# Output projection by seven products of quarters, with weight sums made by adding transfers

## The chip, the cores and the metric

The kernel runs on one core of one Trainium2 chip. The metric is the device time of one execution in microseconds; the kernel before takes 1031.3 us (median of 3 runs, 1031.29 to 1032.03).

The engines have these names: PE multiplies matrices (PEld is its weight load), DVE and ACT work element by element on 128 partitions, POOL does the same more slowly and also issues transfers that can add to what lies at their target, and SP issues plain transfers. Each engine takes its instructions strictly in its own order.

## The reference, cut to what matters

One decoder layer over 512 tokens of width 1024: three token-mixing branches (attention, pooling, state space), gated and summed to `merged`, an output projection, and a gated feed-forward block with its own norm.

```
merged = gates[:, :, 0] * y_a + gates[:, :, 1] * y_b + gates[:, :, 2] * y_c
x = x + merged @ w_o[i]
x = x + conv_ffn(rmsnorm(x, ln2_g[i]), ffn_w_up[i], ffn_conv_w[i], ffn_conv_b[i], ffn_w_down[i])
return rmsnorm(x, final_g)
```

`w_o` is 1024 x 1024, `merged` is 512 x 1024. All values are float32. The kernel splits each operand into a high part (rounded to PE's fp32r) and a low part (the rest), and a product is the sum of high x high, high x low and low x high (`mm3`): three matmuls for each block of 128 rows of the summed dimension.

## The kernel before

The program is a list of jobs. A job has a piece of weights (1 MB at most), a body with its matmuls, and what becomes of the result. While job n multiplies, the weights of job n+1 get their low part (DVE, `low`, line 215), those of job n+2 are cast to their high part (ACT, `cast`, line 195, in two halves), and those of job n+3 are fetched (SP, line 183). So PE's input passes SP, ACT and DVE in turn, one job apart. PE, ACT, DVE and POOL run in the order in which the program was written down (`manual_schedule`); `step()` marks the places in that order where work from other lists (`waiting`, `running`) is put in. The order of the transfers on SP is a scheduler's.

Around the change the jobs are these:

- The third branch (`branch_jobs(2, w_c, ..., last=True)`): four jobs of 48 matmuls, each for two blocks m of 128 columns of `merged`, all 512 tokens wide and transposed. After each block DVE multiplies the product by the gate (line 1265) and adds it to the sum of the other branches (1266), ACT casts the sum to its high part (1269), DVE makes the low part (1270).
- The output projection (`wo_jobs`): for each pair of token blocks (0, 1 and then 2, 3), for each half h of the 1024 output columns, two jobs of 24 matmuls, one for each half of the summed dimension. DVE adds the result to x (line 1291). After half 0 `norm_early` takes the row's squares (ACT) and the product with the norm weights (POOL, line 441). After half 1 `norm_late` finishes the norm: squares (ACT), weights (DVE 450), variance (451), square root (ACT 452), reciprocal and one refinement (454 to 456), scaling of both halves (464). PE then turns the block (`norm_turn`, line 430), ACT and DVE copy it to `uh2`, `ul2`, the input of the feed-forward block.
- The first up-projection jobs (`opening`, line 1493) begin with the token blocks 0 and 1, take in blocks 2 and 3 in the middle, and set off the low parts of their own weights late (`job.late`).

The kernel already uses a scheme of seven products of quarters instead of eight in other places (`sevens` for parts of the input projection, `sevens_down` for the down projection): the tokens are halved (LO, HI), the blocks of the summed dimension are taken in even and odd ones, the output columns are halved. `sums_of` makes the four sums on the side of the tokens and their high and low parts, in three steps that `step()` sets off one after the other.

Of the kernel before, what the change touches and what calls it, by code (L numbers as in the profile page):

```python
# [10 lines left out]
F32 = mybir.dt.float32  # L11
F32R = mybir.dt.float32r
# [71 lines left out]
def trunk(ctx: ExitStack, tc, out, x, rel_bias, ln1_g, w_in, b_gate, w_a, pool_w, pool_scale, w_b,  # L84
# [23 lines left out]
    def T(name, dt=F32, shape=(P, S)):  # L108
        return big.tile(list(shape), dt, name=name, tag="t")
# [323 lines left out]
            act.copy(hh, pv)  # L433
            dve.tensor_sub(ul[:, 4 * h:4 * h + 4, tb * P:(tb + 1) * P], pv, hh.bitcast(F32))

    def norm_early(t, g):

        ss, v0, xg = small("ss", [P, 1]), cpool.tile([P, 1], F32, name=f"v0_{len(V0)}"), T("xg")
        squares(act, t, ss)
        dve.tensor_scalar(v0, ss, 1.0 / D, EPS, OP.mult, OP.add)  # L440
        pool.tensor_tensor(xg, t, g[:, :S], OP.mult)
        V0.append(v0)
        return v0, xg

    def norm_late(t, g, v0, outs, both=False):

        ss, v, sq, r, rt = (small(n, [P, 1]) for n in ("ss", "v", "sq", "r", "rt"))
        squares(act, t, ss)
        xg = T("xg")
        dve.tensor_tensor(xg, t, g[:, S:], OP.mult)  # L450
        dve.scalar_tensor_tensor(v, ss, 1.0 / D, v0, OP.mult, OP.add)
        act.activation(sq, v, AF.Sqrt)
        yield xg
        dve.reciprocal(r, sq)
        dve.scalar_tensor_tensor(rt, r, v, r, OP.mult, OP.mult)
        dve.tensor_scalar(rt, rt, -0.5, 1.5, OP.mult, OP.add)
        if both:
            dve.tensor_tensor(r, r, rt, OP.mult)
            (_, a), (_, b) = outs(xg)
            dve.tensor_scalar(a, a, r, None, OP.mult)  # L460
            act.mul(b, b, r)
            return
        for o, src in outs(xg):
            dve.tensor_scalar(o, src, r, rt, OP.mult, OP.mult)
# [793 lines left out]
    def branch_jobs(b, w, parts, nk, last=False, more=()):  # L1258
        def evac(m, ps):
            if b == 1:  # L1260
                MG[m] = T("yo")
                act.copy(MG[m], ps)
                return
            s = SG[b, m]
            dve.tensor_tensor(s, s, ps, OP.mult)
            (dve if last else pool).tensor_tensor(MG[m], MG[m], s, OP.add)
            if last:
                h, l = T("mgh", F32R), T("mgl", F32R)
                act.copy(h, MG[m])
                dve.tensor_sub(l, MG[m], h.bitcast(F32))  # L1270
                MH[m] = (h, l)

        return jobs_a(w, 0, 8, lambda k: parts[k][0], lambda k: parts[k][1], nk, evac,
                      width=256 if nk > 4 else 512, more=more)


    X1 = {}
    nxt = {}
    late, late_split = [], []

# [4 lines left out]
                t = X1[tb, h] = T("x1")  # L1285
                sp.dma_start(t, x[tb * P:(tb + 1) * P, h * S:(h + 1) * S])

    def wo_jobs(pair, h):
        def evac(tb, ps):
            t = X1[tb, h]  # L1290
            dve.tensor_tensor(t, t, ps, OP.add)
            if h == 0:
                nxt[tb] = norm_early(t, nxt["g2"])
                return
            if "uh" not in nxt:
                nxt["uh"] = upool.tile([P, KD, S], F32R, name="uh2", tag="uh")
                nxt["ul"] = upool.tile([P, KD, S], F32R, name="ul2", tag="ul")
            v0, xg0 = nxt[tb]
            us = [T("u0"), T("u1")]
            it = norm_late(t, nxt["g2"], v0, lambda xg1: ((us[0], xg0), (us[1], xg1)))  # L1300
            next(it)

            def rest():
                next(it, None)
                yield
                norm_turn(us, nxt["uh"], nxt["ul"], tb)

            if pair == 0:
                r = rest()
                next(r)  # L1310
                running.append(after(1, r))
            elif tb == 2:
                r2 = rest()
                next(r2)
                late.append(r2)
            else:
                late.append(rest())
                late_split.pop(0)()

        return jobs_b(lambda k0, k1: [wsrc(w_o, k0, k1, h * S, h * S + S)], S,  # L1320
                      lambda k, tb: MH[k][0][:, tb * P:(tb + 1) * P],
                      lambda k, tb: MH[k][1][:, tb * P:(tb + 1) * P], KD, evac,
                      blocks=(2 * pair, 2 * pair + 1), turn_over=pair == 1 and h == 1)


    ACTS = {}
# [235 lines left out]
    def program():  # L1562
        yield from jobs_a(w_in, C_POOL, 8, uhk, ulk, KD, pool_evac)
        yield Call(lambda: waiting.append(rows_of_bias()))
        yield from v_jobs(0)
        yield from qk_jobs(0)
        yield from pool_out_job()
        yield Call(lambda: attend(0))
        yield Call(lambda: waiting.insert(3, ssd_prep()))
        for i, job in enumerate(branch_jobs(1, w_b, YB, 8, more=range(7))):  # L1570
            if i == 3:
                yield Call(lambda: running.extend(after(p, sums_of_u(p)) for p in range(4)))
            yield job
        load, pair = v_pair()
        Q = lambda i: (C_Q + 384 + i * P, lambda: q_sink(1, i))
        K = lambda i: (C_K + 384 + i * P, lambda: k_sink(1, i))
        G = lambda i, left: (C_GATE + D + i * P, lambda: gate_sink(1, i, left))
        BC = lambda lo, hi, width: jobs_a(w_in, C_XBC + lo * P, hi - lo, uhk, ulk, KD,
                                          lambda m, ps: xbc_evac(lo + m, ps), width)
        loads, s = zip(  # L1580
            set_of_sevens((G(2, True), G(3, True)), (G(4, False), G(5, False)), "a"),
            set_of_sevens((Q(0), Q(1)), (K(0), K(1)), "c", (0.125, 0.125)),
            set_of_sevens((Q(2), G(0, True)), (K(2), G(1, False)), "a", (0.125, 1.0)))
        yield Call(load)
        yield from BC(8, 10, 256)
        yield from gate_jobs(1, 6, 8)
        pair[5].then, pair[6].then, s[0]["four"].then = loads
        yield from pair
        spare = BC(10, 12, P)
        for i, n in ((0, "one"), (0, "five"), (0, "two"), (0, "three"), (0, "six"), (1, "one"),  # L1590
                     (0, "seven"), (1, "five"), (0, "four"), (1, "three"), (1, "two"), (1, "six"),
                     (2, "one"), (1, "seven"), (2, "five"), (1, "four"), (2, "three"), (2, "two"),
                     (2, "six"), (2, "seven"), (2, "four")):
            if (i, n) in ((2, "seven"), (2, "four")):
                yield next(spare)
            yield s[i][n]
        yield Call(settle)
        yield Call(lambda: attend(1))
        yield from BC(0, 8, 256)
        yield Call(ssd_start)  # L1600
        yield from qk_jobs(2)
        yield Call(lambda: attend(2))
        yield Call(lambda: fill([after(2, combine())]))
        yield from gate_jobs(0)
        many = {"a": branch_jobs(0, w_a, AO, 3), "g": gate_jobs(2),
                "Z": z_jobs(0), "z": z_jobs(1)}
        for token in MIX:
            if token in many:
                yield next(many[token])
            else:  # L1610
                yield Call(lambda i=int(token): waiting.append(y_norm(i)))
        yield Call(finish)
        yield from branch_jobs(2, w_c, YT, 8, last=True)
        yield Call(load_x1)
        for pair in range(2):
            for h in range(2):
                yield from wo_jobs(pair, h)
            if pair == 0:
                yield Call(ff_cols)
        first, between, _ = sevens_down(0)  # L1620
        second_, last_, opened = sevens_down(1, keep=True)
        extra = {EARLY + i: between[w] for i, w in enumerate(
            ("two", "one", "five", "three", "six", "seven", "four"))}
        extra.update({LATE + i: last_[w] for i, w in enumerate(("two", "one", "five", "six"))})
        for i, job in enumerate(up_jobs()):
            yield job
            if i == EARLY - 3:
                yield Call(first)
            if i == LATE - 1:
                yield Call(second_)  # L1630
            if i in extra:
                yield extra[i]
        yield Call(lambda: fin.setdefault("g", grow(final_g)))
        yield Call(finish)
        yield from down(last_, opened)
# [181 lines left out]
NBIG = 54  # L1817
MORE = 2
SPLIT = 4
MIX = "ZZ0zz1ggggaa"  # L1820
SSD_ORDER = ((0, 0, 1), (1, 0, 1), (0, 1, 1), (2, 0, 1), (1, 1, 1), (3, 0, 1), (2, 1, 1), (3, 1, 1))
WARM = 19
EARLY, LATE = 8, 18
# [29 lines left out]
```

## Time and profile before

| | before |
|---|---|
| median of the runs | 1031.3 us |
| profiled execution | 1029.93 us |
| its span | 1028.2 us |
| granted PE clock (mean) | 0.999 |
| PE busy | 1019.2 us (99%) |
| DVE busy | 698.6 us (68%) |
| ACT busy | 485.1 us (47%) |
| POOL busy | 161.7 us (16%) |
| third branch | 579.6 to 623.1 us |
| output projection | 623.1 to 669.0 us |

The span counts from the first to the last instruction of the profiled execution; the execution's own time holds a little more. In the lists of instructions a row gives the start in us, the duration (of all in the row, where it ends in x2 or more), the engine, the line, the operation, output and inputs, the shape, and in brackets how long the engine had been idle and what ended that. A matmul row's duration includes its way through the array; what counts is the distance from start to start.

### The profile page before, as it was taken

The numbers are of one execution on the slowest core, as the hardware profiler recorded it, in microseconds if no ns is written. First come the engines' busy times: TensorE is split into PE (matmuls) and PEld (weight loads), VectorE is DVE, ScalarE is ACT, GpSimd is POOL, SyncE is SP. The second block draws the span as 40 slices with busy tenths as digits, with TensorE's granted clock in tenths as the row PEclk, the third lists the DMA queues.
The fourth block names the chain that finished last, engine by engine and source line by source line (L and its number), as shares of the span: only waits on it lengthen the run. The fifth ranks groups of instructions, "written<-read, shape, count | busy, mean of one in ns | idle before, by whom it ended". The sixth has DMA issues, their size and how long they took to land.

```text
span 1028.2 us, 13683 instructions
## 1 busy us (share of the span) xinstructions
PE 1019.2 (99%) x5420; PEld 866.3 (84%) x5420; DVE 698.6 (68%) x938; ACT 485.1 (47%) x811; POOL 161.7 (16%) x135
## 2 busy tenths in 40 slices
PE   9999999999999999999999999999999999999997
PEld 9898878899998888888888888898888888888885
DVE  6553566776867668766768666767768677666775
ACT  6432554456545564548546234544444443443342
POOL 2770000001100005110162501101111001111120
PEclk9999999999999999999999999999999999999999
DMA  8344312156544244452234526543233224323142
GB/s 290 116 132 136 106 58 76 31 121 167 114 123 123 82 125 135 112 142 83 82 115 164 164 82 219 180 141 100 82 121 120 87 83 163 123 84 121 62 144 82
DMA packets 121919, 123.16 MB, mean 120 GB/s; under 512 B 5603, under 2 KB 104230, under 8 KB 121855
## 3 DMA queue, kind: packets, MB, share of 16 engines
q1 hardware_dynamic: 118543, 119.07, 36.9%
q0 software_dynamic: 2720, 2.36, 1.7%
q8 instruction: 42, 0.69, 0.3%
q10 hardware_dynamic: 592, 0.86, 0.2%
q14 instruction: 22, 0.18, 0.1%
HBM read 118.48 MB, written 2.22 MB: 117 GB/s over the span
## 4 chain that ended last, share of the span: by engine, by line
PE 98%; DVE 1%; ACT 0%; issue 0%; DVEq 0%; ACTq 0%
PE pa L234 32%; PE pu L234 22%; PE p L234 17%; PE pb L234 8%; PE pqk L234 6%; PE pa L1704 2%; PE ps L808 1%; PE pu L1493 1%; PE ppw L234 1%; PE pt L836 1%; PE po L849 1%; PE py L1134 1%; PE pa L1661 1%; PE pyo L1141 1%; PE pst L1120 0%; PE pxs L1088 0%
## 5 line engine op out<-in xcount | busy, mean ns | idle before, releaser
L215 DVE TENSOR_TENSOR wl<-raw,wh 128x2048 fp32r<-128x2048 f32 (+3 forms) x94 | 208.6, 2221 | 46.0 <-ACT wh L195 35.6
L195 ACT CAST wh<-raw 128x1024 fp32r<-128x1024 f32 (+3 forms) x186 | 180.8, 993 | 45.6 <-DVE raw L339 26.1
L1354 DVE SCALAR_TENSOR_TENSOR hc<-pu,fcol,hc 128x510 f32<-128x510 f32 x88 | 65.8, 748 | 61.1 <-ACT hc L1351 59.5
L234 PE MATMUL pa<-uh,wh 128*128 128x512 f32 x336 | 86.5, 399 | 0.0
L234 PE MATMUL pu<-uh,wl 128*128 128x512 f32 (+1 forms) x352 | 83.7, 380 | 0.0
L234 PE MATMUL pu<-uh,wh 128*128 128x512 f32 (+1 forms) x352 | 83.5, 379 | 0.0
L234 PE MATMUL pu<-ul,wh 128*128 128x512 f32 (+1 forms) x352 | 83.5, 379 | 0.0
L234 PE MATMUL pa<-ul,wh 128*128 128x512 f32 x336 | 83.0, 389 | 0.0
L234 PE MATMUL pa<-uh,wl 128*128 128x512 f32 x336 | 83.0, 389 | 0.0
L234 PEld LDWEIGHTS pu<-uh,wl 128*128 128x128 f32 x352 | 64.1, 188 | 12.8 <-DVE wl L215 0.3
L234 PEld LDWEIGHTS pu<-ul,wh 128*128 128x128 f32 x352 | 64.2, 188 | 12.5
L234 PEld LDWEIGHTS pu<-uh,wh 128*128 128x128 f32 x352 | 64.1, 188 | 12.4
L1359 POOL TENSOR_TENSOR hc<-hc 128x512 f32<-128x512 f32 x22 | 30.4, 1382 | 278.9 <-DVE hc L1354 243.9
L234 PEld LDWEIGHTS pa<-ul,wh 128*128 128x128 f32 x336 | 63.1, 188 | 13.3
L234 PEld LDWEIGHTS pa<-uh,wl 128*128 128x128 f32 x336 | 63.1, 188 | 13.1
L234 PEld LDWEIGHTS pa<-uh,wh 128*128 128x128 f32 x336 | 61.2, 188 | 12.8 <-issue 1.0
L1351 ACT ACTIVATE hc<-pu,fcol,fcol 128x512 f32<-128x512 f32 x40 | 31.2, 780 | 81.3 <-PE pu L234 81.0
L829 ACT ACTIVATE sb<-sb,both 128x128 f32<-128x128 f32 (+1 forms) x72 | 30.1, 418 | 31.8 <-DVE both L826 21.7
L195 ACT CAST wh<-w 128x512 fp32r<-128x512 f32 (+2 forms) x50 | 35.4, 748 | 17.7 <-DVE w L349 8.8
L370 POOL DMA_DIRECT2D w<-in_w_in_dram x10 | 12.3, 1230 | 199.3 <-DVE w L349 147.5
L215 DVE TENSOR_TENSOR wl<-w,wh 128x1024 fp32r<-128x1024 f32 (+2 forms) x25 | 38.5, 1540 | 6.5 <-ACT wh L195 4.4
L1356 ACT ACTIVATE hc<-hc 128x512 f32<-128x512 f32 x22 | 13.9, 632 | 42.7 <-DVE hc L1354 42.7
(381 smaller groups left out, 1945.0 us busy)
## 6 DMA issues: line engine op xcount, KB each, us to landing
raw<-in_ffn_w_up_dram SPq DMA_DIRECT2D x22, 1024.0 KB
raw<-in_w_in_dram SPq DMA_DIRECT2D x21, 1024.0 KB
raw<-in_ffn_w_down_dram SPq DMA_DIRECT2D x11, 1024.0 KB
raw<-in_w_in_dram SPq DMA_DIRECT2D x20, 512.0 KB
raw<-in_w_o_dram SPq DMA_DIRECT2D x8, 1024.0 KB
raw<-in_w_b_dram SPq DMA_DIRECT2D x4, 1024.0 KB
al<-ad SPq DMA_DIRECT2D x16, 256.0 KB
w<-in_ffn_w_down_dram SPq DMA_DIRECT2D x4, 1024.0 KB
```

Source lines behind the costliest of these rows:

```text
L195: act.copy(job.high[:, :, o], job.raw[:, :, o])
L215: (eng or dve).tensor_tensor(l[:, :, o], job.raw[:, :, o], h[:, :, o].bitcast(F32), OP.subtract)
L234: pe.matmul(ps, l, r, start=first and n == 0, stop=last and n == total - 1, skip_group_check=again)
L370: pool.dma_start(W[1][:, k:k + 2, at:at + n], src[:, k:k + 2, :], accum_op=OP.add)
L808: pe.matmul(pss[i][:, o:o + w * P], q[r, n * P:(n + 1) * P], k[r, kb * P:(kb + w) * P], start=True, stop=True)
L829: act.activation(sb[:, off:off + w * P], sb[:, off:off + w * P], AF.Exp, bias=nm[:, n, h:h + 1], accum_out=ls[:, n, h:h + 1])
L836: pe.transpose(pt[:, o:o + P], sb[:, o:o + P], eye)
L1351: act.activation(t, ps, AF.Identity, bias=ff["c1"][:, ff["b"] + m:ff["b"] + m + 1], scale=fw(2, m))
L1354: dve.scalar_tensor_tensor(t[:, sh:], ps[:, :S - sh], fw(k, m), t[:, sh:], OP.mult, OP.add)
L1356: act.activation(t, t, AF.Silu)
L1359: pool.tensor_tensor(a, a, t, OP.mult)
L1704: pe.matmul(first[2 * n + j][:, lo:hi], a[:, k, j * P:(j + 1) * P], b[:, k, lo:hi], start=a is wh and b is uh and k == 0, stop=a is wl and ...
```

## The change

The output projection becomes seven jobs of 24 matmuls, `wo_sevens`, in place of eight. They run in the order one, two, five, three, six, seven, four. With the token halves (LO: blocks 0, 1; HI: blocks 2, 3), "one" and "two" give half 0 of the columns for LO, "five" and "seven" half 1 for HI, "three" and "six" add half 1 for LO, "four" half 0 for HI. "One", "six", "seven" and "four" add up in the same two PSUM banks X, "five" and "three" in Z; after each product DVE adds the bank to x, or subtracts it (`plus`), and PE goes on adding into the bank.

On the side of the tokens, the third branch's blocks come in pairs. After the even block only its LO half is cast and gets a low part; after the odd one the whole block, and then `sums_of` runs for the pair, its steps set off by `step()` in the following jobs. The last pair's steps fall into "one" and "two".

On the side of the weights four sums of quarters are needed. "Five" and "six" start as plain 1 MB loads into the tile of the first norm's output `uh`, which is free after the last gate product, "seven" and "four" as loads into two other tiles. Eight transfers issued by POOL add onto them (`accum_op`), two for each: other quarters from memory, and then "five" into "six" and "six" into "four". Only "one", "two" and "three" still fetch weights on SP as jobs.

`norm_early` and `norm_late` take the half of the columns that comes first or last as an argument. For blocks 2 and 3 half 1 now comes first. One of the two scalings of a normed block goes to ACT (`both=True`), the other stays on DVE, and a 1-column product is added on DVE. The loads of x move ahead by one job of the third branch; the loads of the first w_down tiles, which stood on SP among the w_c loads, now follow the projection's low parts, because the tiles are used for "seven" and "four" first. The matmuls of the projection go from 192 to 168.

```
-            (_, a), (_, b) = outs(xg)
-            dve.tensor_scalar(a, a, r, None, OP.mult)
-            act.mul(b, b, r)
+            (o, a), (p, b) = outs(xg)
+            dve.tensor_scalar(o, a, r, None, OP.mult)
+            act.mul(p, b, r)
...
             if last:
+                if m % 2 == 0:
+                    t = T("mga", F32R)
+                    act.copy(t[:, :256], MG[m][:, LO])
+                    dve.tensor_sub(t[:, 256:], MG[m][:, LO], t[:, :256].bitcast(F32))
+                    MS["A11", m // 2] = (t[:, :256], t[:, 256:])
+                    return
                 h, l = T("mgh", F32R), T("mgl", F32R)
                 act.copy(h, MG[m])
                 dve.tensor_sub(l, MG[m], h.bitcast(F32))
-                MH[m] = (h, l)
+                for j, half in (("A12", LO), ("A22", HI)):
+                    MS[j, m // 2] = (h[:, half], l[:, half])
+                running.append(sums_of(MG[m - 1], MG[m], T("sah", F32R), T("sal", F32R),
+                                       lambda j, h, l, p=m // 2: MS.__setitem__((j, p), (h, l)), -1))
...
-    def wo_jobs(pair, h):
...
+    def wo_sevens():
+
+        q = lambda two, h: w_o[:, h * S:h * S + S].rearrange("(k two p) c -> two p k c", two=2, p=P)[two]
+        W, X, Y, Z, r = {}, {}, {}, {}, {}
+
+        def load():
+            both_ = upool.tile([P, KD, S], F32R, name="ws", tag="uh").bitcast(F32)
+            W["five"], W["six"] = both_[:, :4, :], both_[:, 4:, :]
+            sp.dma_start(W["five"], q(0, 0))
+            sp.dma_start(W["six"], q(1, 1))
+
+        def add():
+            for name, src in (("seven", q(0, 1)), ("four", q(1, 0))):
+                W[name] = ypool.tile([P, 4, S], F32, name="w3", tag="xs")
+                sp.dma_start(W[name], src)
+            for name, src in (("five", q(0, 1)), ("seven", q(1, 1)), ("six", W["five"]),
+                              ("four", W["six"])):
+                for k in (0, 2):
+                    pool.dma_start(W[name][:, k:k + 2, :], src[:, k:k + 2, :], accum_op=OP.add)
+
+        def plus(tb, h, what, op=OP.add):
+            dve.tensor_tensor(X1[tb, h], X1[tb, h], what, op)
+
+        def late_norm(tb, h):
...
+            it = norm_late(X1[tb, h], nxt["g2"], v0, lambda xg1: ((us[1 - h], xg0), (us[h], xg1)),
+                           True, h)
+            next(it)
+
+            def rest():
+                next(it, None)
+                yield
+                norm_turn(us, nxt["uh"], nxt["ul"], tb)
+            return rest()
+
+        def use(name, i):
+            if name == "one":
+                plus(i, 0, X[i])
+            elif name == "two":
+                plus(i, 0, Y[i])
+                nxt[i] = norm_early(X1[i, 0], nxt["g2"])
+            elif name == "five":
+                plus(2 + i, 1, Z[i])
+            elif name == "three":
+                plus(i, 1, Z[i])
+            elif name == "six":
+                plus(i, 1, X[i], OP.subtract)
+                r[i] = late_norm(i, 1)
+                if i:
+                    next(r[0])
+                    next(r[1])
+            elif name == "seven":
+                plus(2 + i, 1, X[i], OP.subtract)
+                nxt[2 + i] = norm_early(X1[2 + i, 1], nxt["g2"], 1)
+                next(r[i], None)
             else:
+                plus(2 + i, 0, X[i])
+                r[i] = late_norm(2 + i, 0)
+                late.append(r[i])
+                if i == 0:
+                    next(r[i])
+                else:
+                    late_split.pop(0)()
+
+        banks = {"one": X, "six": X, "seven": X, "four": X, "five": Z, "three": Z, "two": Y}
...
+                for i in range(2):
+                    o = slice(i * P, (i + 1) * P)
+                    mm3(banks[name][i], lambda k: wh[:, k, :], lambda k: wl[:, k, :],
+                        lambda k: parts[k][0][:, o], lambda k: parts[k][1][:, o], range(4),
+                        fresh, True, flip=True, again=not fresh)
+                    use(name, i)
+                    if i:
+                        step()
...
-        yield from branch_jobs(2, w_c, YT, 8, last=True)
-        yield Call(load_x1)
-        for pair in range(2):
-            for h in range(2):
-                yield from wo_jobs(pair, h)
-            if pair == 0:
+        yield Call(add)
+        for i, job in enumerate(branch_jobs(2, w_c, YT, 8, last=True)):
+            if i == 3:
+                yield Call(load_x1)
+            yield job
+        for i, job in enumerate(output):
+            yield job
+            if i == 3:
                 yield Call(ff_cols)
...
-MIX = "ZZ0zz1ggggaa"
+MIX = "ZZ0zz1ggggWaa"
```

More of the change, by code (lines that the diff above doesn't have):

```diff
@@ L434, in norm_turn, with norm_early @@
             dve.tensor_sub(ul[:, 4 * h:4 * h + 4, tb * P:(tb + 1) * P], pv, hh.bitcast(F32))
-    def norm_early(t, g):
+    def norm_early(t, g, h=0):
         ss, v0, xg = small("ss", [P, 1]), cpool.tile([P, 1], F32, name=f"v0_{len(V0)}"), T("xg")
@@ L440, in norm_early, with norm_late @@
         dve.tensor_scalar(v0, ss, 1.0 / D, EPS, OP.mult, OP.add)
-        pool.tensor_tensor(xg, t, g[:, :S], OP.mult)
+        pool.tensor_tensor(xg, t, g[:, h * S:h * S + S], OP.mult)
         V0.append(v0)
         return v0, xg
-    def norm_late(t, g, v0, outs, both=False):
+    def norm_late(t, g, v0, outs, both=False, h=1):
         ss, v, sq, r, rt = (small(n, [P, 1]) for n in ("ss", "v", "sq", "r", "rt"))
@@ L449, in norm_late @@
         xg = T("xg")
-        dve.tensor_tensor(xg, t, g[:, S:], OP.mult)
+        dve.tensor_tensor(xg, t, g[:, h * S:h * S + S], OP.mult)
         dve.scalar_tensor_tensor(v, ss, 1.0 / D, v0, OP.mult, OP.add)
@@ L1270, in evac @@
                 dve.tensor_sub(l, MG[m], h.bitcast(F32))
-                MH[m] = (h, l)
+                for j, half in (("A12", LO), ("A22", HI)):
+                    MS[j, m // 2] = (h[:, half], l[:, half])
+                running.append(sums_of(MG[m - 1], MG[m], T("sah", F32R), T("sal", F32R),
+                                       lambda j, h, l, p=m // 2: MS.__setitem__((j, p), (h, l)), -1))
         return jobs_a(w, 0, 8, lambda k: parts[k][0], lambda k: parts[k][1], nk, evac,
                       width=256 if nk > 4 else 512, more=more)
-    X1 = {}
+    MS, X1 = {}, {}
     nxt = {}
@@ L1286, in load_x1 @@
                 sp.dma_start(t, x[tb * P:(tb + 1) * P, h * S:(h + 1) * S])
-    def wo_jobs(pair, h):
[L1289 to L1294, printed above, removed]
+    def wo_sevens():
[17 more added lines that the diff above has]
+        def late_norm(tb, h):
             if "uh" not in nxt:
@@ L1306, in rest @@
                 norm_turn(us, nxt["uh"], nxt["ul"], tb)
-            if pair == 0:
[L1309 to L1315, printed above, removed]
-            else:
[L1317 to L1323, printed above, removed]
+            return rest()
@@ new lines, in wo_sevens, with make, body @@
+        banks = {"one": X, "six": X, "seven": X, "four": X, "five": Z, "three": Z, "two": Y}
+        jobs = {}
+        def make(name, source=None):
+            def body(ws):
+                wh, wl = ws
+                parts = [MS[SIDES[name], p] for p in range(4)]
+                fresh = name in ("one", "two", "five")
+                if name == "four":
+                    late_split.append(jobs[name].prepare(later=True))
+                if name == "one":
+                    for i in range(2):
+                        Y[i] = MM("p2")
+                    for i in range(2):
+                        X[i] = MM("p1")
+                if name == "five":
+                    for i in range(2):
+                        Z[i] = SM("p5")
+                for i in range(2):
+                    o = slice(i * P, (i + 1) * P)
[5 more added lines that the diff above has]
+                        step()
+            job = jobs[name] = Job([source] if source is not None else [], 4, S, body)
+            if source is None:
+                job.load = lambda: None
+                job.form = lambda: W[name]
+            job.late = name == "four"
+            return job
@@ L1326, in trunk @@
+        return load, add, [make("one", q(0, 0)), make("two", q(1, 0)), make("five"),
+                           make("three", q(1, 1)), make("six"), make("seven"), make("four")]
     ACTS = {}
@@ L1606, in program @@
                 "Z": z_jobs(0), "z": z_jobs(1)}
+        load, add, output = wo_sevens()
         for token in MIX:
-            if token in many:
+            if token == "W":
+                yield Call(load)
+            elif token in many:
                 yield next(many[token])
@@ L1612, in program @@
         yield Call(finish)
-        yield from branch_jobs(2, w_c, YT, 8, last=True)
-        yield Call(load_x1)
-        for pair in range(2):
-            for h in range(2):
-                yield from wo_jobs(pair, h)
-            if pair == 0:
+        yield Call(add)
[6 more added lines that the diff above has]
+            if i == 3:
                 yield Call(ff_cols)
```

1 line of the change is left out of this document (removed).

## The prediction

> **What bounds the kernel now.** I read the page's busy times first, then the chain that ended last, then the stretches of the stage that the change touches, then the instructions there in order of time.
>
> ```profile
> PE 1019.2 (99%) x5420; PEld 866.3 (84%) x5420; DVE 698.6 (68%) x938; ACT 485.1 (47%) x811; POOL 161.7 (16%) x135
> PE 98%; DVE 1%; ACT 0%; issue 0%; DVEq 0%; ACTq 0%
> ```
>
> ```profile
> core 0: us, PE busy (x) PEld busy (x) DVE busy (x) ACT busy (x) POOL busy (x), PEclk, DMA share, GB/s
> 612.20:623.10 10.90, 10.90 (x49) 9.01 (x48) 6.43 (x7) 3.15 (x4) 0.00 (x0) 1.00 0.39 127
> 623.10:669.00 45.90, 45.90 (x212) 37.98 (x211) 31.98 (x46) 23.84 (x38) 5.18 (x4) 1.00 0.57 198
> ```
>
> PE is busy for 99% of the span and is 98% of the chain. In the output projection (623.1 to 669.0 us) it has no gap either, while DVE works 32.0 of 45.9 us and ACT 23.8. So whatever PE loses is lost at the end, and whatever PE saves is a gain only while DVE and ACT keep up in their own order. These are PE's rows at both ends of that stage:
>
> ```profile
> 617.67 1.98 PE L234 MATMUL pa<-yth,wh 128*128 128x512 f32 x8
> ...
> 623.12 1.07 PE L234 MATMUL pb<-wh,mgh 128*128 128x512 f32 x4
> ...
> 668.95 2.08 PE L1493 MATMUL pu<-uh,wh 128*128 128x256 f32 x16
> 670.87 2.08 PE L1493 MATMUL pu<-ul,wh 128*128 128x256 f32 x16
> 672.79 1.04 PE L430 MATMUL uT<-eye,u 128*128 128x128 f32 x8
> 673.86 2.18 PE L1493 MATMUL pu<-uh,wl 128*128 128x256 f32 x16
> ```
>
> From 617.67 to 623.12 lie 24 matmuls: 0.227 us each at this pace (the listed 389 ns of one is its latency). A 256-wide one costs 1.92/16 = 0.12, a transpose about 0.11.
>
> **What the change takes from PE.** Eight jobs of 24 matmuls become seven: 24 x 0.227 = 5.44 us. Were that all, the time would be 1025.9. One weight split (cast and low part) and one 1 MB fetch by a job fall away with it.
>
> **What it adds beside PE.** The prices, from DVE, ACT and POOL:
>
> ```profile
> 623.31 0.69 DVE L1265 TENSOR_TENSOR sg<-sg,pa 128x512 f32<-128x512 f32 x1 [2.58 <-PE pa L234]
> 625.49 0.69 DVE L1270 TENSOR_TENSOR mgl<-yo,mgh 128x512 fp32r<-128x512 f32 x1 [0.69 <-ACT mgh L1269]
> 626.44 4.66 DVE L215 TENSOR_TENSOR wl<-raw,wh 128x2048 fp32r<-128x2048 f32 x2 [0.26 <-ACT wh L195]
> 631.48 0.69 DVE L1291 TENSOR_TENSOR x<-x,pb 128x512 f32<-128x512 f32 x1 [0.37 <-PE pb L234]
> 632.95 0.15 DVE L440 TENSOR_SCALAR v<-ss 128x1 f32<-128x1 f32 x1 [0.79 <-ACT junk L417]
> ...
> 671.52 2.29 DVE L215 TENSOR_TENSOR wl<-raw,wh 128x2048 fp32r<-128x2048 f32 x1
> ```
>
> ```profile
> 635.55 3.88 ACT L195 CAST wh<-raw 128x1024 fp32r<-128x1024 f32 x4
> ...
> 651.59 2.04 ACT L433 CAST uh<-uT 128x512 fp32r<-128x512 f32 x4
> ```
>
> ```profile
> L324 DVE TENSOR_TENSOR sa<-hc x8: 412/415/420, 707.5 to 898.0; 128x256 f32<-128x256 f32 x8
> L333 DVE TENSOR_TENSOR sal<-sa,sah x12: 679/681/685, 190.4 to 908.9; 128x512 fp32r<-128x512 f32 x12
> L461 ACT ACTIVATE xg<-xg,r x1: 722/722/722, 1023.7 to 1023.7; 128x512 f32<-128x512 f32 x1
> ```
>
> In the third branch each pair of row blocks adds six DVE operations, four of 256 columns (1.5 us together) and two of 512 (1.3), less 0.3 for the halved low part: 2.5 us on DVE per job of 10.9, where it works 6.4 now. ACT adds 1 us there. For the first three pairs PE covers that. The last pair's work falls into the projection.
>
> I now lay the built order of the new program out on before's clock from 623.12 us, with these durations: low part 2.29 (the next operation starts 0.09 before its end), a sum into x 0.69, square and its read 0.71, half a cast 0.95, and DVE starting 0.2 after PE's last matmul.
>
> (a) Block 7's product ends at 623.1. DVE then does gate product, sum and low part (to 626.2), the low parts of pair 2's sums (627.4), four sums of pair 3 (628.8), and only then "two"'s weight low part: 628.7 to 631.0. "One" ends at 628.56, and "two" asks for it eight matmuls later, at 630.37. PE waits 0.7.
>
> (b) DVE goes on with two sums into x, "five"'s low part (632.1 to 634.4), the first sum from "two" (635.0), a wait for ACT's square (635.8), the second sum (636.6), a second such wait (637.5), and then the low part of pair 3's sums. "Five" starts at 634.7 and asks for that with its eighth matmul, at 636.3. Beside it POOL multiplies the second x by the norm weights, 636.6 to 638.0. What two such operations do to each other, the trace shows once:
>
> ```profile
> 697.90 1.29 POOL L1359 TENSOR_TENSOR hc<-hc 128x512 f32<-128x512 f32 x1 [0.33 <-DVE hc L1354]
> 698.04 1.42 DVE L1377 TENSOR_TENSOR f<-hc,f 128x256 fp32r<-128x256 f32 x1 [0.31 <-ACT f L1376]
> L1377 DVE TENSOR_TENSOR f<-hc,f x8: 412/414/1424, 698.0 to 887.2; 128x256 fp32r<-128x256 f32 x8
> ```
>
> The DVE operation, 0.41 elsewhere, ended 0.27 us after POOL's. So I let the low part begin when POOL is done and end at 638.7: PE waits 2.5 us (1.9 without this). [...] "Three" then has its low part and its banks in time (PE 642.6 to 648.1), and "six" runs to 653.5.
>
> (c) The norm of blocks 0 and 1. The built order puts both sums from "six", both products with the norm weights and both variances on DVE ahead of the first reciprocal: second sum 653.7, ACT's square 654.5 to 655.2, variance 655.4, then four small operations and the scaling, to 656.7. PE, done with half of "seven" at 656.2, waits 0.5 before it turns block 0.
>
> (d) ACT scales the second halves (656.2 and 657.5, by 0.72 each) and only then casts "four"'s weights, 658.1 to 660.1. DVE's low part of "four" waits for that (660.2 to 662.5), and behind it, in DVE's order, stands the sum that reads "seven"'s first bank, whose product was complete at 656.2. "Four" adds into that same bank, so PE, free at 661.2, waits until 663.1: 1.9 us. (e) The second bank's sum stands behind ACT's square and the copies of the turned block 0: 666.3 instead of 665.8, 0.5 us.
>
> (f) DVE then has block 1's turned low parts, the first sum from "four" (668.8 to 669.5), its norm behind ACT's casts for the first up product (they end at 670.0), the second sum (672.5), its norm weights and variance (to 674.1), and then that up product's low part, 674.0 to 676.3. PE, which needs it at 674.1, waits 2.3. Before, the same operation ended at 673.81 and PE started at 673.86.
>
> The sum to that point. After: 168 x 0.227 = 38.1, 24 transposes 2.6, columns 0.3, 32 narrow matmuls 3.8, waits 0.7 + 2.5 + 0.5 + 1.9 + 0.5 + 2.3 = 8.4: 53.2 us, so 676.4 where before has 673.86: 2.5 us later. The next 1 MB fetch, freed by that low part, and the casts behind it move along (before: fetch at 673.87, cast at 678.95). After this PE had no waits before and gains nothing back. So 1028.2 + 2.5 = 1030.7 for the span, 1029.9 + 2.5 = 1032.4 for the profiled execution, and 1031.3 + 2.5 = 1033.8 for the median, which lies 1.4 above the profiled run.
>
> **Transfers, costed at nothing, and their cover.** POOL takes over eight adding transfers of 512 KB. The kernel has ten smaller ones:
>
> ```profile
> L370 POOL DMA_DIRECT2D w<-in_w_in_dram x10: 1204/1212/1362, 204.7 to 282.4; - x10
> DMA to landing us min/median/max: 3.5/4.6/6.4
> ```
>
> ```profile
> 274.77 1.21 POOL L370 DMA_DIRECT2D w<-in_w_in_dram  x1 [2.58 <-issue]
> 278.54 1.20 POOL L370 DMA_DIRECT2D w<-in_w_in_dram  x1 [2.56 <-issue]
> ...
> 580.56 3.27 POOL L1266 TENSOR_TENSOR yo<-yo,sg 128x512 f32<-128x512 f32 x1 [0.60 <-DVE sg L1265]
> ```
>
> POOL is free for them from 583.8. At 3.8 us from one to the next the last is issued after 27 us; at twice that (twice the bytes), after 53, at 637, landing by 643. "Five"'s two come first and have landed by 598 even then; its cast is at 626. "Four"'s, the last, is cast at 658. Behind them on POOL stand the two norm products of 635 and 637, read at 656. SP gains two 1 MB loads into the freed u tile (after the last gate product, 563.4) and one second w_c fetch behind them. The second of the two fetches in the row below was issued at 566.8 and its cast began at 571.9, 5.1 us for 1 MB, so it would now land near 579; its product starts at 590.5:
>
> ```profile
> 571.89 2.00 ACT L195 CAST wh<-raw 128x1024 fp32r<-128x1024 f32 x2 [4.02 <-DMA raw<-in_w_c_dram]
> ...
> 559.93 7.20 SPq L183 DMA_DIRECT2D raw<-in_w_c_dram  x2
> ```
>
> The w_down loads that stood there go behind "four"'s low part on SP, still ahead of the first w_down job; the x loads start earlier, and the fetch for "three" behind them lands near 625 and is cast at 637.
>
> **Rivals.**
> 1. The saving is kept. PE would never wait for DVE: 1031.3 - 5.4 = 1025.9. For it: PE has no gap in the earlier stages that use seven products, and DVE is only 70% busy here. Against: those do not have a norm between the products. To end faster by more than 0.2% (2.06 us, about the least that a measurement of this kernel can tell from no change), the low part of (f) must end by 671.7, 4.6 us ahead of my layout. That takes (a) and (b) gone (3.2) and most of (d) too: if DVE and ACT pass waits on faster than the rows say. Chance 0.12.
> 2. The waits are there but smaller, so that they about eat the saving: without (a) and (b) the layout gives 2.5 - 3.2 = -0.7, 1030.6; without POOL's share in (b) alone, about 2.0. Anything 0.5 to 4.6 us short of my sum lies here. Chance 0.32.
> 3. An adding transfer is the new wait. It decides if one takes over 9 us of POOL's queue (658 less 584, by eight); at 12 us the last ends 22 us too late, near 1055. The spacing of 3.8 speaks against it. Chance 0.03.
> 4. PE slows down after these waits; the granted clock is 1.00 all through this stage now, so no row prices it. [...] Chance 0.03.
>
> **How the numbers follow.** My layout 0.50, rival 2 0.32, rival 1 0.12, rivals 3 and 4 0.06. Slower by over 0.2%: 0.56; within: 0.32; faster: 0.12. The range goes from 1029.2, where "within" begins, to 1036.8: three more microseconds than my sum, as every wait passes through several engines and could be half a microsecond longer. It leaves out rival 1 and rivals 3 and 4, 0.18.
>
> **What will show it.** In the new profile: 24 fewer matmuls; PE gaps ended by DVE ahead of "two"'s low-part matmuls (0.7), in "five" (2.5), before "four"'s first bank (1.9) and before the first up product's low-part matmuls (2.3); that low part ending near 676.3; POOL's transfers done by 643; no gap of PE in the third branch. I am wrong if PE enters the up product without a gap, if the largest gap is ended by a DMA, or if the clock is below 1.00.

## The result, and the profile after

The changed kernel takes 1034.01 us (median of 9 runs, 1032.28 to 1035.44), the kernel before 1031.30 us (9 runs, 1030.61 to 1032.03): a ratio of 1.0024, with an interval of 1.0014 to 1.0034. It is slower, by 2.7 us, where 1033.8 was forecast. The profiled execution took 1034.79 us, its span 1033.0 us.

First the page's busy times of the changed kernel, and its stretches (columns as in the prediction, PEclk is the third last):

```profile
PE 1017.7 (99%) x5396; PEld 863.3 (84%) x5396; DVE 707.6 (69%) x967; ACT 489.4 (47%) x821; POOL 170.0 (16%) x143
```

```profile
612.20:623.10 10.90, 10.90 (x50) 9.03 (x49) 8.63 (x13) 4.01 (x7) 1.73 (x2) 1.00 1.06 278
623.10:669.00 45.90, 41.46 (x180) 32.92 (x178) 33.05 (x49) 22.41 (x35) 4.70 (x4) 0.96 0.52 163
...
641.30:644.71 3.41, 3.41 (x10) 2.63 (x9) 2.35 (x2) 1.32 (x2) 0.00 (x0) 0.50 0.07 18
```

PE issues 24 matmuls fewer. In the third branch it still has no gap, though DVE's work there went from 6.43 to 8.63 us. In the projection 4.4 us of PE have become idle, and the granted clock is 0.96 where it was 1.00: it is 0.50 for 3.4 us, from 641.3 to 644.7.

The waits of PE that are new against the profile before, from the view of waits (engine, tile and line, what ended the wait: us in total, times, longest):

```profile
PE p L234 <- DVE sal L333: 1.9, 1, 1.9
PE pu L1569 <- DVE wl L215: 1.6, 1, 1.6
PE p L234 <- DVE x L1318: 1.6, 1, 1.6
PE p L234 <- DVE wl L215: 1.1, 2, 0.6
...
PE uT L430 <- DVE r L454: 0.4, 1, 0.4
```

One of the two waits for `wl` of line 215 stands at 240.11 us, where nothing was changed. It comes in six of the ten profiles of this study, less24's below among them, and is no part of this account. Where the others stand, in PE's rows in order of time:

```profile
624.62 1.98 PE L234 MATMUL p<-wh,mga 128*128 128x512 f32 x8
...
632.59 1.20 PE L234 MATMUL p<-wl,mgh 128*128 128x512 f32 x4 [0.56 <-DVE wl L215]
...
640.04 0.50 PE L234 MATMUL p<-wh,sal 128*128 128x512 f32 x1 [1.92 <-DVE sal L333]
640.37 1.13 PE L234 MATMUL p<-wl,sah 128*128 128x512 f32 x4
641.30 1.91 PE L234 MATMUL p<-wh,sah 128*128 128x512 f32 x4
643.01 1.86 PE L234 MATMUL p<-wh,sal 128*128 128x512 f32 x4
644.71 1.07 PE L234 MATMUL p<-wl,sah 128*128 128x512 f32 x4
...
659.78 1.06 PE L430 MATMUL uT<-eye,u 128*128 128x128 f32 x8 [0.41 <-DVE r L454]
...
666.06 1.16 PE L234 MATMUL p<-wh,mgh 128*128 128x512 f32 x4 [1.55 <-DVE x L1318]
...
679.07 2.18 PE L1569 MATMUL pu<-uh,wl 128*128 128x256 f32 x16 [1.63 <-DVE wl L215]
```

Every gap of PE in this stage ends at DVE, and none at a transfer. From the projection's first matmul (624.62) to the first up product's low-part matmuls (679.07) lie 54.45 us; before, 50.74 (623.12 to 673.86). This stretch, called the stage below, is 3.7 us longer, and 1.6 of that is the clock: the eight matmuls from 641.30 to 644.71 took 3.41 us instead of 8 x 0.227 = 1.82. The 1.5 us by which the projection starts later are there already when the third branch starts (581.10 against 579.60; the branch takes 43.5 us in both). A difference of that size comes without the change too: the kernel before with matmuls left out, below, starts its third branch at 581.05 and its projection at 624.58. Behind the stage the changed kernel is 0.4 us shorter (353.9 us to the end of the span against 354.3, and 353.9 in the repeat below), all of it after PE's last matmuls; its cause is not known.

The engines behind these waits: DVE's rows, then POOL's and ACT's.

```profile
630.25 2.29 DVE L215 TENSOR_TENSOR wl<-raw,wh 128x2048 fp32r<-128x2048 f32 x1
...
638.95 1.04 DVE L333 TENSOR_TENSOR sal<-sa,sah 128x512 fp32r<-128x512 f32 x1
...
658.25 0.16 DVE L454 RECIPROCAL r<-sq 128x1 f32<-128x1 f32 x1
...
663.02 2.29 DVE L215 TENSOR_TENSOR wl<-w,wh 128x2048 fp32r<-128x2048 f32 x1 [2.08 <-ACT wh L195]
665.23 0.68 DVE L1318 TENSOR_TENSOR x<-x,p 128x512 f32<-128x512 f32 x1
...
668.45 0.68 DVE L1318 TENSOR_TENSOR x<-x,p 128x512 f32<-128x512 f32 x1
...
676.73 2.29 DVE L215 TENSOR_TENSOR wl<-raw,wh 128x2048 fp32r<-128x2048 f32 x1
```

```profile
585.28 1.23 POOL L1315 DMA_DIRECT2D ws<-in_w_o_dram  x1
...
623.67 0.86 POOL L1315 DMA_DIRECT2D w<-ws  x1 [4.75 <-DMA ws<-ws]
...
638.17 1.26 POOL L441 TENSOR_TENSOR xg<-x,grow 128x512 f32<-128x512 f32 x1 [0.27 <-DVE x L1318]
```

```profile
654.77 0.63 ACT L417 ACTIVATE junk<-x 128x512 f32<-128x512 f32 x1 [7.82 <-DVE x L1318]
...
661.01 1.98 ACT L195 CAST wh<-w 128x1024 fp32r<-128x1024 f32 x2
```

"Two"'s weight low part (630.25) ends at 632.54, and PE goes on at 632.59. The sum's low part (`sal`) takes 1.04 us beside POOL's product and 0.68 elsewhere, and PE resumes when it is done. "Four"'s low part (663.02) waits for ACT's cast of 661.01, and behind it at 665.23 stands the sum that frees "four"'s first bank, at 668.45 the one that frees its second; ACT had been idle for 7.8 us before 654.77, so that cast is late by its place in the order, not for want of time. Block 0's reciprocal (658.25) comes only behind block 1's variance on DVE, and PE turns block 0 at 659.78. The first up product's low part runs from 676.73. The last adding transfer is issued at 623.67.

### The profile page after: what moved, and what is told of

Its sections match the earlier page's. It is cut to its first block, busy times and chain, and to the rows that moved or that the text cites. A ratio compares the mean times of both kernels' runs of the same rounds, so it can differ in the third digit from the quotient of the medians.

```text
span 1033.0 us, 13696 instructions
## 1 busy us (share of the span) xinstructions
PE 1017.7 (99%) x5396; PEld 863.3 (84%) x5396; DVE 707.6 (69%) x967; ACT 489.4 (47%) x821; POOL 170.0 (16%) x143
## 5 line engine op out<-in xcount | busy, mean ns | idle before, releaser
L215 DVE TENSOR_TENSOR wl<-raw,wh 128x2048 fp32r<-128x2048 f32 (+3 forms) x89 | 197.2, 2217 | 40.4 <-ACT wh L195 31.1
L195 ACT CAST wh<-raw 128x1024 fp32r<-128x1024 f32 (+3 forms) x176 | 170.9, 990 | 44.5 <-DVE raw L339 26.1
L215 DVE TENSOR_TENSOR wl<-w,wh 128x1024 fp32r<-128x1024 f32 (+2 forms) x27 | 43.1, 1596 | 10.5 <-ACT wh L195 8.4
L195 ACT CAST wh<-w 128x512 fp32r<-128x512 f32 (+2 forms) x54 | 39.4, 770 | 22.8 <-DVE w L349 10.3
```

The source lines that it names most:

```text
L195: act.copy(job.high[:, :, o], job.raw[:, :, o])
L215: (eng or dve).tensor_tensor(l[:, :, o], job.raw[:, :, o], h[:, :, o].bitcast(F32), OP.subtract)
```

## The experiments

All ratios are against the kernel before on the same chip: 1031.30 us (9 runs) for the changed kernel's row, 1030.95 us (22 runs) for repeat to cast_early, 1031.33 us (26 runs) for fill to four_low_on_pool. These are different chips, so across the groups compare ratios and not medians. "Stage" is the stretch defined above in each one's profile.

| kernel | median, us (runs) | ratio, interval | stage, us |
|---|---|---|---|
| before | | | 50.74 |
| changed | 1034.01 (9) | 1.0024 (1.0014 to 1.0034) | 54.45 |
| repeat | 1032.84 (11) | 1.0022 (1.0013 to 1.0031) | 52.88 |
| no_adds | 1034.16 (6) | 1.0027 (1.0015 to 1.0040) | 52.87 |
| sums_early | 1035.35 (5) | 1.0040 (1.0028 to 1.0053) | 55.58 |
| cast_early | 1031.95 (11) | 1.0012 (1.0003 to 1.0020) | 52.34 |
| fill | 1033.10 (11) | 1.0018 (1.0009 to 1.0027) | 52.91 |
| less24 | 1029.10 (11) | 0.9979 (0.9970 to 0.9988) | 48.74 |
| three | 1028.29 (8) | 0.9972 (0.9962 to 0.9982) | 48.45 |
| four_low_on_pool | 1027.79 (7) | 0.9970 (0.9959 to 0.9981) | 47.44 |

**repeat: the changed kernel once more.** No edit.

> The changed kernel again, to stand beside the others on the same chip. Theory (PE waits for DVE and ACT, whose order puts urgent work behind less urgent work; after the 1.9 us wait in five the granted clock falls for some 3.4 us in most runs, which costs about 1.6 more): about 1034 us, the runs in two groups some 2 us apart by their granted clock (0.997 and 0.998 to 0.999). Rival (spread of the chip alone): one group, the clock the same in all.

PE's rows in its profiled execution:

```profile
624.03 1.98 PE L234 MATMUL p<-wh,mga 128*128 128x512 f32 x8
...
639.46 0.50 PE L234 MATMUL p<-wh,sal 128*128 128x512 f32 x1 [1.95 <-DVE sal L333]
...
640.72 1.08 PE L234 MATMUL p<-wh,sah 128*128 128x512 f32 x4
...
676.91 2.17 PE L1569 MATMUL pu<-uh,wl 128*128 128x256 f32 x16 [1.68 <-DVE wl L215]
```

The waits are the same to 0.05 us, but here no slow matmuls follow the 1.95 us: the clock fell in one execution and not in the other. Without the fall the stage is 2.1 us longer than before. The mean clock of each run agrees with that. In the first nine runs of the changed kernel, six have 0.997 and average 1034.5 us, three have 0.998 or 0.999 and average 1032.4; here three have 0.997 (average 1034.4) and eight 0.998 or 0.999 (1032.7). A loss of 1.6 us is 0.0016 of 1031, about the difference in clock and most of the difference in time. The mean clock is not a sharp mark, though: one of the eight took 1034.1, and the kernel before shows 0.997 in 2 of 48 runs.

**no_adds: without the adding transfers.**

```
             for name, src in (("five", q(0, 1)), ("seven", q(1, 1)), ("six", W["five"]),
                               ("four", W["six"])):
-                for k in (0, 2):
-                    pool.dma_start(W[name][:, k:k + 2, :], src[:, k:k + 2, :], accum_op=OP.add)
+                pass
```

> Leaves out the eight adding transfers, so four of the seven products use wrong weights. Theory: the transfers are covered; the same waits of PE, within 0.7 us of the repeated kernel. Rival (the transfers' 4 MB, or POOL's work for them, hold up casts, DVE or PE): 2 us or more faster, and the waits in five and four shorter.

This kernel leaves out the sums of the weights. It takes 1034.16 us, 1.3 more than the repeat and not within the 0.7 expected; but four of its six runs have a mean clock of 0.997, and in the repeat three of eleven. Its profiled execution, where the clock did not fall, has the same waits (0.56, 1.94, 0.41, 1.58, 1.67) and the same stage as the repeat's, 52.87 against 52.88. So the eight transfers cost nothing on PE's path.

**sums_early: the steps of the last pair's sums one place earlier.**

```
-                    if i:
+                    if i or name == "one":
                         step()
```

The added `step()` also sets off other work that waits in its lists, casts among it.

> The last pair's sums get their high parts after the first half of one and their low parts before five's weights are split, instead of after two. Theory (queue order): the wait in five goes, but three's weight low part on DVE still waits for ACT's late cast and stands ahead of the sum that frees three's bank, so PE waits there instead, 2 to 3.3 us; no faster than the repeated kernel by over 1 us. Rival (this one operation is the cause): the wait is gone for good, 1.9 us faster, 3.5 with the clock, so 1030.5 to 1032.

PE's rows:

```profile
644.50 1.27 PE L234 MATMUL p<-wh,sbh 128*128 128x512 f32 x4 [3.06 <-DVE x L1318]
645.57 1.91 PE L234 MATMUL p<-wh,sbl 128*128 128x512 f32 x4
647.28 1.79 PE L234 MATMUL p<-wl,sbh 128*128 128x512 f32 x4
648.91 1.09 PE L234 MATMUL p<-wh,sbh 128*128 128x512 f32 x4
```

and DVE's:

```profile
641.47 2.29 DVE L215 TENSOR_TENSOR wl<-raw,wh 128x2048 fp32r<-128x2048 f32 x1 [1.73 <-ACT wh L195]
643.67 1.28 DVE L1318 TENSOR_TENSOR x<-x,p 128x512 f32<-128x512 f32 x2
```

The wait in "five" is gone, so it was a matter of place in the order. But a longer one stands at "three", 3.06 us, ended by the first of the sums of 643.67, which takes "five"'s result out of the bank: it stands behind the low part for "three", and that now waits for ACT's cast. The clock fell after it, and all five runs have 0.997.

**cast_early: the casts for "three", "six", "seven" and "four" as soon as the job two ahead begins**, instead of both halves being set aside for its later steps.

```
+            job.now = name in ("three", "six", "seven", "four")
...
-                        cast(weights[n + 2], 2, spread=not later)
+                        cast(weights[n + 2], 2, spread=not (later or weights[n + 2].now))
```

> The casts for three, six, seven and four are issued at the start of the job two before, not at its end. Theory: ACT casts four's weights in its idle time before the norm, so DVE's low part of four and the sum behind it come 2 us sooner; the wait before four (1.6) goes, the one in five stays; about 2.2 us faster than the repeated kernel, near 1032. Rival (the norm chain of the last blocks sets the end whatever happens before): the wait before the first up product grows by as much, no faster.

PE's rows:

```profile
640.38 0.50 PE L234 MATMUL p<-wh,sal 128*128 128x512 f32 x1 [1.94 <-DVE sal L333]
640.72 1.46 PE L234 MATMUL p<-wl,sah 128*128 128x512 f32 x4
641.98 1.91 PE L234 MATMUL p<-wh,sah 128*128 128x512 f32 x4
...
664.62 1.17 PE L234 MATMUL p<-wh,mgh 128*128 128x512 f32 x4
```

The wait ahead of "four" (664.62) is gone, the one in "five" and the fall behind it are as they were. With the same fall, the stage is 2.1 us shorter than the changed kernel's: that wait and the smaller one at "four"'s second bank, 1.72 and 0.28 us from start to start (below). The late cast was the cause of step (d) of the prediction. In time the gain is smaller than the 2.2 expected: the median is 0.9 below the repeat's. Seven of these eleven runs have a mean clock of 0.996 or less, against three of eleven with 0.997 in the repeat; among the others the average is 1031.5 against 1032.7.

**fill: eight matmuls of no use in the wait of "five"**, into a bank that nothing reads, ahead of its eighth matmul.

```
...
+                            if n_ == 7:
+                                for f in range(8):
+                                    pe.matmul(fill, parts[0][0][:, o], wh[:, 0, :], start=True, stop=True)
...
```

> Eight extra matmuls into an unused bank are put into PE's wait in five (8 x 0.227 = 1.8 us of the 1.9 measured); everything else as in the changed kernel. Theory (the idle PE is what lets the granted clock fall): no run at 0.997, all runs near 1032.3, though PE does more work. Rival (the fall has another cause, and comes in some runs anyway): two groups of runs as before, near 1032.4 and 1034.3.

```profile
638.31 1.98 PE L1392 MATMUL fill<-wh,sah 128*128 128x512 f32 x8
640.44 0.50 PE L1393 MATMUL p<-wh,sal 128*128 128x512 f32 x1 [0.16 <-DVE sal L333]
...
641.70 1.09 PE L234 MATMUL p<-wh,sah 128*128 128x512 f32 x4
```

With PE busy, the operand arrives no earlier, the clock stays at 1.00, and none of eleven runs has 0.997. So the idle time itself brings the fall. The stage is 52.91, that of the repeat without a fall. The time is hardly better (a ratio of 1.0018, 1.0022 in the repeat), and the runs are not all near the 1032.3 expected: they spread from 1031.8 to 1034.2 us, so the clock explains only a part of the spread from run to run.

**less24: the kernel before with 24 matmuls left out.** Six of the 16 half products (four matmuls for the low part of the weights each) of token blocks 0 and 1 are dropped; every other engine does what it did.

```
-        n, total = 0, 3 * len(ks)
-        for a, b in ((wh, xh), (wh, xl), (wl, xh)):
+        n, total = 0, (2 if two else 3) * len(ks)
+        for a, b in ((wh, xh), (wh, xl), (wl, xh))[:2 if two else 3]:
...
+                      short=((0, 4), (0,))[h] if pair == 0 else ())
```

> The kernel before, without the low x high group in six of the projection's sixteen half products: 24 matmuls fewer, every other instruction kept; the output loses some of its last bits. Theory: the saving by itself, 24 x 0.227 = 5.4 us, so 1025.5 on this chip. Rival (DVE or ACT stand right behind PE here, so that a shorter PE stage opens waits of its own): less than 4 us faster.

PE's rows, then ACT's:

```profile
624.58 1.07 PE L234 MATMUL pb<-wh,mgh 128*128 128x512 f32 x4
...
637.37 1.21 PE L234 MATMUL pb<-wh,mgh 128*128 128x512 f32 x4 [1.75 <-ACT wh L195]
...
673.32 2.18 PE L1494 MATMUL pu<-uh,wl 128*128 128x256 f32 x16
```

```profile
635.12 0.19 ACT L417 ACTIVATION_READ_ACCUMULATOR junk<-x 128x1 f32 x1
635.32 1.99 ACT L195 CAST wh<-raw 128x1024 fp32r<-128x1024 f32 x2
```

Of 24 x 0.227 = 5.4 us only 2.2 come back (2.0 in the stage): the rival of the expectation holds, and not its theory. PE, ahead of its time, meets ACT's cast, which stands behind the norm's squares; two waits take 1.75 and 0.19 us, and most of the rest is in gaps of 0.1 to 0.3 us at the start of groups of matmuls. The kernel before already ran close to what its other engines can feed here, before any sums were added. All 24 were taken from the first two token blocks, so the 2.2 us hold for that place; another choice was not run.

**three: the three causes mended together.** The edits of sums_early and cast_early, and "five"'s work on the next weights' low part put behind the sum that frees its bank.

```
+                    if name == "five" and i == 0:
+                        jobs[name].prepare()
+                    if i or name == "one":
                         step()
...
-            job.late = name == "four"
+            job.late = name in ("five", "four")
+            job.now = name in ("three", "six", "seven", "four")
```

> The early low parts of the last pair's sums, the early casts, and three's weight low part behind the sum that frees three's bank. Theory: PE's waits in five, three and before four are gone; 0.6 in two, 0.4 before the turn and some 1.7 to 2.3 before the first up product's low-part matmuls stay; 2 us faster than the kernel before, 1029. Rival (the end is set by the norms of blocks 2 and 3 alone): the last wait grows, no faster than 1031.

```profile
671.97 2.18 PE L1572 MATMUL pu<-uh,wl 128*128 128x256 f32 x16 [1.64 <-DVE wl L215]
```

1028.29 us, 3.0 less than before (0.9972, 0.9962 to 0.9982), all eight runs at a clock of 0.998 or 0.999. The waits in "five", at "three" and ahead of "four" are gone together; 0.56 at "two", 0.41 at the turning, and the 1.64 shown are left.

**four_low_on_pool: as three, with the first up product's cast earlier and its low part on POOL.**

```
+                    job.now = job.pool = half == 0
...
+                        if weights[n + 1].pool:
+                            low(weights[n + 1], 4, pool)
+                        else:
+                            low(weights[n + 1])
```

> As the one before, and the first up product's low part moves from DVE to POOL, its cast to before the norms of blocks 2 and 3. Theory: the last wait (1.7 to 2.3) goes too if POOL is done with 2048 columns within some 8 us; 1027 to 1027.5. Rival (POOL and DVE block one another on operations with two inputs in memory): DVE's norm products or POOL's low part stretch, and it is no faster than the one before.

PE's rows, then POOL's, then DVE's:

```profile
671.32 1.09 PE L430 MATMUL uT<-eye,u 128*128 128x128 f32 x8 [0.67 <-ACT u L461]
672.17 2.16 PE L1572 MATMUL pu<-uh,wl 128*128 128x256 f32 x16
...
679.50 2.18 PE L1572 MATMUL pu<-uh,wl 128*128 128x256 f32 x16 [0.46 <-DVE wl L215]
```

```profile
664.64 5.48 POOL L215 TENSOR_TENSOR wl<-raw,wh 128x512 fp32r<-128x512 f32 x4
```

```profile
666.41 1.30 DVE L450 TENSOR_TENSOR xg<-x,grow 128x512 f32<-128x512 f32 x1
667.64 1.24 DVE L451 SCALAR_TENSOR_TENSOR v<-ss,v 128x1 f32<-128x1 f32 x1
```

1027.79 us (0.9970, 0.9959 to 0.9981). The 1.6 us wait is gone, but the norm of block 2 is now late by 0.67 us and the next low part by 0.46. The rival of the expectation fits the first: beside POOL's low part (to 670.12) DVE's product with the norm weights takes 1.30 us and the variance 1.24, in the changed kernel 0.69 and 0.16 each of eight times. The median is 0.5 below that of three, but their runs overlap (1027.67 to 1028.63 against 1027.61 to 1028.56, averages 0.2 apart), so no gain in time over three is shown.

## Why the prediction was right, and where not

The sign and the way there were right: the saving of 5.4 us is more than eaten by PE's waits for DVE. That the time came out so close (1033.8 forecast, 1034.01 measured) is in part luck. The three runs of the changed kernel whose mean clock shows no fall average 1032.4 us, 1.1 above the kernel before and not 2.5; such runs of the repeat lie 1.75 above theirs. The 1032.4 is 1.4 us short of the sum, inside what the forecast gave to rival 2. The fall of the clock, which the forecast held at 0.03, came in six of the nine runs by their mean clock and brought the median up to the forecast.

In the stage alone the layout was nearer: 2.1 us longer than before in the repeat, where 2.5 was forecast; the 0.4 us gained behind the stage, where it gave nothing back, is the other part. The steps measured waits from where PE's next matmul would have started. So taken, the changed kernel's rows give these (for "five" as an example, 637.73, the start of the last matmul ahead, + 0.227 to 640.04 is 2.08):

| step | forecast, us | measured, us |
|---|---|---|
| (a) "two" waits for its weight low part | 0.7 | 0.71 |
| (b) "five" waits for the sum's low part | 2.5 | 2.08 |
| (c) turning block 0 | 0.5 | 0.56 |
| (d) "four"'s first bank | 1.9 | 1.72 |
| (e) "four"'s second bank | 0.5 | 0.28 |
| (f) the up product's low part | 2.3 | 1.80 |
| sum | 8.4 | 7.15 |

- Each wait was in its place and had the cause that the prediction gave it. Shown by an edit are (b), by sums_early and three, (d), by cast_early, and (f), by four_low_on_pool, where the wait is gone from the rows though not clearly from the time. (e) went with (d) in cast_early; (a) and (c) rest on the rows alone.
- (b) and (f) were sized too long. In (b) the low part was held up by POOL's product for 0.6 us in the forecast; in the trace the two overlap for 0.48 (638.95 to 639.43), and DVE's operation is 0.36 longer than elsewhere (1.04 against 0.68). That it would begin only when POOL was done was the author's estimate. No run leaves POOL's product out, so its share of the wait is read and not tested. The step's other 0.2 us, and why (f) fell short by 0.5, were not traced further.
- Left out of the sum: PE does not resume at full pace. The first four matmuls after the wait in "two" take 1.04 us from start to start and not 0.91, and so, by about 0.1, at each restart (in the kernel before, also behind transposes without a wait: 1.01). The forecast's 44.8 us of work and 7.15 of waits leave 0.9 us to the 52.85 that were measured (the changed kernel's 54.45 less the 1.6 of the clock); some 0.7 of it is at such places. So waits that were 1.25 too long and restarts that were missing cancel in the most part, and the forecast had 53.2.
- Rival 4, the fall of the clock, was wrongly held at 0.03. That the clock would hold was the author's estimate, with no row behind it: the longest wait of PE in the kernel before is 1.1 us. The clock fell after a wait of 1.92 us, to 0.50 for the eight matmuls from 641.30 to 644.71, and cost 1.6 us. The forecast's own mark for being wrong, a clock below 1.00, was met.
- Transfers at nothing: right, by no_adds. The spacing on POOL was longer than 3.8 (38.4 us for seven steps, from 585.28 to 623.67, 5.5 each on average), inside the limit of 9 named in rival 3, and the last was issued 13 us ahead of the 637 allowed.
- Rival 1, that the saving is kept, was wrong, and less24 shows that the added sums are not the only reason: 24 matmuls fewer in the kernel before, with nothing added, give only 2.2 us of 5.4. Rival 2, smaller waits, is right for the waits (1.25 us shorter in all) and for the runs without a fall, but in the median the restarts and the clock took that back.

Open is why the clock falls after the same wait in one execution and not in another, and what makes the part behind the stage 0.4 us shorter.

## What to carry to other kernels

Before a product is shortened on a saturated engine, lay out the other engines' queues in their order from the point where it gets shorter: an operation that PE needs stands behind work that waits for a third engine, and each such place is a wait (here 1.92 us in "five" and 1.55 ahead of "four"). Leaving matmuls out without adding anything shows in one run how much of the saving the side work lets through as it stands, for the place where they are left out; three, with a better order, got more (3.0 us against 2.2). Waits of this kind give way to a change of place, as in "three", but mending one alone can lengthen the next, as in sums_early (3.06 us at "three" once the 1.92 in "five" was gone), so mend them together.

## What the hardware showed that was not expected

- The granted clock fell to half (0.50 in the changed kernel) after an idle time of 1.92 to 1.95 us, in some executions: among the four profiles with this wait it fell in two and held in two. After 3.06 us (one profile, and by their clock all five runs) it fell, after 1.55 to 1.75 us it held in each profile (less24, with its 1.75, has two of eleven runs at 0.996 and 0.997, no longer than the rest and without a profile). It fell about 1 us after PE had resumed and stayed so for some 3.4 us (in the changed kernel 1.26 us after 640.04, and for 3.41 us). What decides whether it falls after the same wait, no run here shows.
- Eight adding transfers of 512 KB behind one another on POOL are issued 5.5 us apart on average (0.7 to 8.2), with POOL idle in between (4.75 us ahead of the last, until the transfer that makes its source had landed).
- Three of DVE's operations took longer beside one of POOL's: 1.04 us and not 0.68 for the sum's low part in the changed kernel, and in four_low_on_pool 1.30 and not 0.69 for the product with the norm weights, 1.24 and not 0.16 for the variance.
